# A hybrid attention and RG-LRU block on one core: where weight subtractions and key projections stand in the attention

## Chip, core and metric

One Trainium2 chip, one of its cores. The metric is the device time of one execution in microseconds (us). Each time is a median over runs; the profile is one execution of its own.

## What is computed

One trunk layer in float32, for 512 tokens of width 1024, 16 heads of width 64 and a feed-forward width of 2816:

```python
xn = rmsnorm(h, norm_mix_g)
u = einsum('bsd,de->bse', xn, w_in)
q, k, v, xr, gr, ga, gb = split(u, 7 parts of 1024)
ya = chunked_band_attention(q, k, v, rel_table) @ w_attn_out
xc = causal_depthwise_conv(xr, conv_w, conv_b)
hr = rg_lru(xc, w_rg_r, b_rg_r, w_rg_i, b_rg_i, rg_lambda)
yb = (hr * gelu(gr)) @ w_rnn_out
g_a, g_b = split(sigmoid(concat([ga, gb]) + b_merge))
h = h + (g_a * ya + g_b * yb) @ w_o
hn = rmsnorm(h, norm_ffn_g)
g, up = split(hn @ w_ffn_in)
h = h + (silu(g) * up) @ w_ffn_out
out = rmsnorm(h, final_norm_g)
```

## The kernel before

Every float32 operand of a matmul is split into a high and a low part: ScalarE copies the high part (L82), VectorE subtracts it from the source (L83), and each product is three matmuls (L76 to L78). Weights come from HBM into `raw` tiles by SyncE's queue (SP, L143), and are split into `whl` tiles. One chunk of weights, such as `qk3` (the columns of q and k of head pair 3) or `ga0` (two column blocks of gate A), is two loads and two splits, for rows 0 to 511 (`_0`) and 512 to 1023 (`_4`). There are four `whl` buffers, so room for two chunks: the splits of a chunk wait until the one before the last has been used up. The order of chunks is `plan`; a call of `weights` fetches one chunk ahead of the one it returns.

The stage in question is the attention. It goes through 16 heads, two to a pair. For head h, TensorE does, in this order, which is fixed by hand (`manual_schedule` for TensorE):

- `transposed(h)`: ten transposes of the probabilities `p` into `pT`, which are split into `pp`;
- `scores(h + 1)`: eight matmuls of `q` with the high and low keys `kh` and `kl`. VectorE adds the bias and takes the running minimum (L733), ScalarE takes exponentials (L734), VectorE the reciprocal `rl` of their sums (L735), and GpSimd scales the four blocks of `p` by it (L737);
- the projections that `laid[h]` names ahead of the bar;
- `weigh(h)`: eight matmuls of `pp` with the values, collected in `oacc`; after the second head of a pair the result is split into `aT`;
- the projections that `laid[h]` names behind the bar.

The projections are matmuls that need nothing from the softmax and fill its latency: `q_tile` and `k_tile` of the later pairs, and `gate_a`, the gate's columns. Each is 24 matmuls of 512 columns. The result of `k_tile` goes through two steps on ScalarE, one on VectorE and one on GpSimd for each head of the pair: `kh` (L693), `kl` (L694), and copies of both into the other half of the partitions (L695, L696).

Beside this, the stage prepares the feed-forward's Strassen-like block products: sums and differences of weight blocks are made once on VectorE and kept in HBM. `spill` loads four blocks of `w_ffn_out` (tiles `spill_a2` and `spill_a3`), subtracts them (L607) and stores them (L609, L611); `spill_in` does the like for two chunks of `w_ffn_in` (`spill_fg2`, `spill_fu2`, L632 to L636). The loop over heads takes one step of these generators per head, from head 2 on.

TensorE's order is written by hand. On the other engines and on SP's queue the order is set by a scheduler that models the time, and an instruction for which `keep_in_program_order` was called keeps its place in the written order against what is written around it. Before, that is said of the loads of these blocks alone, so the scheduler was free to put the subtractions elsewhere.

## Time and profile before

| what | value |
|---|---|
| time, median of 3 runs | 869.23 us (869.2 to 869.92) |
| time of the profiled execution | 870.58 us |
| its span | 868.6 us |
| mean granted TensorE clock | 0.991 |
| TensorE busy | 847.8 us, 98% of the span |
| VectorE busy | 676.7 us, 78% |
| ScalarE busy | 520.7 us, 60% |
| GpSimd busy | 116.7 us, 13% |
| DMA | 147.23 MB, 169 GB/s |

A row of the list of waits reads: engine, what waits, line, `<-` the one it waits for: total us, times, longest us. In a timeline a row is start, duration, engine, line, operation, out<-in, shape, count, and in brackets the idle time before it and what ended it. Names are those of tiles in the code, with the numbers left out (`spill_a` is `spill_a2` and `spill_a3`).

### The profile page before, as it was taken

To read this page: it belongs to the slowest core of one execution; us is meant where nothing else is said; L and a number is where in the kernel's file an instruction comes from. 1 tells how busy PE (TensorE), PEld (TensorE's weight loads), DVE (VectorE), ACT (ScalarE), POOL (GpSimd) and SP (SyncE) were. 2 spreads that over 40 slices of the span, in tenths; PEclk is the share of its full clock that TensorE was granted. 3 is DMA by queue.
4 is the path that set the end of the run, shared out by engine and by line. 5 is a ranking of instruction groups with operands and counts; after the bars stand their busy time and mean duration, and the time that the engine had idled before them with its cause. 6 is when DMAs were issued, how large, how long until landed. Compare 5 with 4: busy or idle time off the path is not lost.

```text
span 868.6 us, 13104 instructions
## 1 busy us (share of the span) xinstructions
PE 847.8 (98%) x4860; PEld 740.7 (85%) x4860; DVE 676.7 (78%) x1006; ACT 520.7 (60%) x893; POOL 116.7 (13%) x152
## 2 busy tenths in 40 slices
PE   8999999999997799999999999999999999999997
PEld 6977887888885688888888889999999999988885
DVE  5789766798677766565658886989999887689985
ACT  7578677625564667666654456655565565385454
POOL 2323302210021424231200000000000001000002
PEclk9999999999998899999999999999999999999999
DMA  8684333684677622232337461365766232886622
GB/s 271 205 304 146 97 97 95 223 331 152 194 225 267 197 64 86 72 111 72 99 110 248 153 216 49 120 238 163 254 207 238 94 122 98 282 291 207 215 72 97
DMA packets 107599, 147.23 MB, mean 169 GB/s; under 512 B 7184, under 2 KB 77440, under 8 KB 107536
## 3 DMA queue, kind: packets, MB, share of 16 engines
q1 hardware_dynamic: 103856, 138.74, 48.6%
q10 hardware_dynamic: 3680, 7.67, 2.9%
q8 instruction: 38, 0.62, 0.3%
q14 instruction: 25, 0.20, 0.1%
HBM read 123.27 MB, written 23.11 MB: 169 GB/s over the span
## 4 chain that ended last, share of the span: by engine, by line
PE 92%; DMA 3%; ACT 2%; DVE 1%; issue 1%; POOL 1%; SPq 0%; ACTq 0%; POOLq 0%; DVEq 0%
PE po_out L76 4%; PE po_out L77 4%; PE po_out L78 4%; PE p_fu L78 2%; PE p_fg L78 2%; PE p_fu L76 2%; PE p_fg L76 2%; PE p_fg L77 2%; PE p_fu L77 2%; PE o L768 2%; PE po_gb L76 2%; PE po_gb L77 2%; PE po_ga L76 2%; PE po_ga L78 2%; PE po_ya L76 2%; PE po_gb L78 2%
## 5 line engine op out<-in xcount | busy, mean ns | idle before, releaser
L737 POOL TENSOR_SCALAR p<-p,rl 128x128 f32<-128x128 f32 (+1 forms) x64 | 44.6, 714 | 104.1 <-DVE rl L735 104.0
L1223 POOL TENSOR_TENSOR act_lo<-act,act_hi 128x1024 fp32r<-128x1024 f32 x1 | 2.4, 2407 | 294.3 <-ACT act_hi L1222 294.3
L734 ACT ACTIVATE p<-p,m 128x128 f32<-128x128 f32 (+1 forms) x64 | 35.7, 563 | 9.1 <-DVE m L733 9.1
L83 DVE TENSOR_TENSOR pp<-pT,pp 128x384 fp32r<-128x384 f32 (+1 forms) x48 | 27.7, 596 | 13.9 <-ACT pp L82 13.8
L83 DVE TENSOR_TENSOR whl_t<-raw_t,whl_t 128x1024 fp32r<-128x1024 f32 x26 | 31.9, 1228 | 0.3 <-ACT whl_t L82 0.3
L733 DVE CUSTOM_DVE_ANT_0 p<-s,bias 128x128 f32<-128x128 f32 (+1 forms) x64 | 29.0, 484 | 1.9 <-PE s L730 1.8
L729 PE MATMUL s<-kh,q 128*128 128x128 f32 (+1 forms) x64 | 22.1, 366 | 7.9 <-ACT kh L695 7.9
L76 PE MATMUL po_gr<-xnT,whl_gr 128*128 128x512 f32 (+1 forms) x80 | 28.2, 353 | 0.1
L82 ACT ACTIVATE whl_t<-raw_t 128x1024 fp32r<-128x1024 f32 x26 | 27.2, 1046 | 1.5 <-PE po_h L78 1.5
L77 PE MATMUL po_xr<-xnT,whl_xr 128*128 128x512 f32 (+1 forms) x80 | 27.8, 353 | 0.0
L77 PE MATMUL po_gr<-xnT,whl_gr 128*128 128x512 f32 (+1 forms) x80 | 27.6, 346 | 0.0
L78 PE MATMUL po_gr<-xnT,whl_gr 128*128 128x512 f32 (+1 forms) x80 | 27.5, 348 | 0.0
L78 PE MATMUL po_xr<-xnT,whl_xr 128*128 128x512 f32 (+1 forms) x80 | 27.3, 346 | 0.0
L76 PE MATMUL po_xr<-xnT,whl_xr 128*128 128x512 f32 (+1 forms) x80 | 26.7, 352 | 0.6 <-ACT xnT L358 0.6
L83 DVE TENSOR_TENSOR whl_fg_s<-s_fg,whl_fg_s 128x1024 fp32r<-128x1024 f32 x20 | 24.4, 1223 | 2.9 <-ACT whl_fg_s L82 2.9
L83 DVE TENSOR_TENSOR whl_fu_s<-s_fu,whl_fu_s 128x1024 fp32r<-128x1024 f32 x20 | 24.4, 1222 | 2.9 <-ACT whl_fu_s L82 2.9
L76 PE MATMUL po_q<-xnT,whl_qk 128*128 128x512 f32 x64 | 26.2, 409 | 0.0
L77 PE MATMUL po_q<-xnT,whl_qk 128*128 128x512 f32 x64 | 25.8, 403 | 0.0
L82 ACT ACTIVATE whl_fu_s<-s_fu 128x1024 fp32r<-128x1024 f32 x20 | 21.0, 1056 | 7.8 <-PE q_fu L78 2.6
L78 PE MATMUL po_q<-xnT,whl_qk 128*128 128x512 f32 x64 | 25.7, 401 | 0.0
L76 PE MATMUL po_gb<-xnT,whl_gb 128*128 128x512 f32 x64 | 25.3, 395 | 0.2 <-DVE xc L497 0.2
L748 PE MATMUL pT<-ident,p 128*128 128x128 f32 x160 | 21.9, 277 | 3.6 <-POOL p L737 3.5
(472 smaller groups left out, 3306.2 us busy)
## 6 DMA issues: line engine op xcount, KB each, us to landing
raw_fg<-in_w_ffn_in_dram SPq DMA_DIRECT2D x22, 512.0 KB, 3.8
raw_fu<-in_w_ffn_in_dram SPq DMA_DIRECT2D x22, 512.0 KB, 3.6
raw_t<-sums SPq DMA_DIRECT2D x20, 512.0 KB, 4.2
raw_qk<-in_w_in_dram SPq DMA_DIRECT2D x32, 256.0 KB, 3.1
raw_b<-in_w_ffn_out_dram SPq DMA_DIRECT2D x15, 512.0 KB, 4.8
spillf<-in_w_ffn_out_dram SPq DMA_DIRECT2D x12, 512.0 KB, 8.4
sums<-spillf SPq DMA_DIRECT2D x12, 512.0 KB, 3.7
raw_xr<-in_w_in_dram SPq DMA_DIRECT2D x8, 512.0 KB, 4.8
```

Of the source, the lines that this page charges most:

```text
L76: pe.matmul(o, sh, mh, start=start, stop=False, skip_group_check=parts)
L77: pe.matmul(o, sh, ml, start=False, stop=False, skip_group_check=parts)
L78: pe.matmul(o, sl, mh, start=False, stop=stop, skip_group_check=parts)
L82: act.activation(hi, src, AF.Copy)
L83: dve.tensor_sub(lo, src, f(hi))
L729: pe.matmul(scs[qb], qs, kh[:, e, 0:w], start=True, stop=False)
L733: dve.tensor_tensor_reduce(prob[qb][:], scs[qb], bias[:, S - w:S], -1.0, 3e38, ALU.add, ALU.min, nmax[:, qb:qb + 1])
L734: act.activation(prob[qb][:], prob[qb][:], AF.Exp, bias=nmax[:, qb:qb + 1], scale=-1.0, accum_out=lsum[:, qb:qb + 1])
L737: pool.tensor_scalar(prob[qb][:], prob[qb][:], rl[:, qb:qb + 1], 1.0, ALU.mult, ALU.mult)
L748: pe.transpose(pt[:, at * P:(at + 1) * P], prob[qb][:, kb * P:(kb + 1) * P], ident[:])
L768: pe.matmul(po[:, S - n:S], st, pp[i][:, part, lo:lo + n], start=kb == 0 and part == 0, stop=kb == NT - 1 and part == 1)
L1223: pool.tensor_sub(lo[:], o[:], f(hi[:]))
```

## The change

Three things. The subtractions of the feed-forward weights keep their written place on VectorE, and the loop gives each generator its own heads (`steps_at`): the loads of `w_ffn_out` at head 1, its four subtractions at heads 3 to 6; the loads of fg2 at head 6 and of fu2 at head 7, their sums at heads 7 and 8, and 9 and 10. The list of projections has q2 behind head 0 and every key projection one head sooner; gates take up the places that come free at the end. The order of weight chunks has `ga2` after `qk7` instead of after `qk6`, to fit the list.

```diff
-        for at, n in ((5, 0), (6, 2), (7, 4), (7, 6)):
+        for at, n in ((5, 0), (7, 2), (7, 4), (7, 6)):
...
-            dve.tensor_sub(out_, a_, b_)
+            in_order(dve.tensor_sub(out_, a_, b_), pinned and w is w_ffn_out)
...
-    def spill_in(name, both):
+    def spill_in(name, at):
         col = chunks[index[name]][1][0][1]
+        both = big(at, [P, 2, 4, CW], F32, f"spill_{name}")
...
         yield
-        dve.tensor_add(s1, s3, s1)
+        in_order(dve.tensor_add(s1, s3, s1), True)
         dve.tensor_sub(s3, s2, s3)
         yield
-        dve.tensor_sub(s2, s1, s2)
+        in_order(dve.tensor_sub(s2, s1, s2), True)
         dve.tensor_sub(s4, s4, s2)
...
-    laid = ("q1 k1 |", "q2 |", "k2 |", "q3 |", "k3 |", "q4 |", "k4 |", "q5 | g0",
-            "k5 | g1", "q6 |", "k6 | g2", "q7 | g3", "k7 | g4", "g5 |", "g6 |", "g7 |")
+    laid = ("q1 k1 | q2", "k2 |", "q3 |", "k3 |", "q4 |", "k4 |", "q5 |", "k5 | g0",
+            "q6 | g1", "k6 |", "q7 |", "k7 | g2", "g3 |", "g4 |", "g5 |", "g6 | g7")
...
-        yield from spill_in("fg2", big(2, [P, 2, 4, CW], F32, "spill_fg2"))
-        yield from spill_in("fu2", big(3, [P, 2, 4, CW], F32, "spill_fu2"))
-
-    spilling = spills()
+
+    spilling = {n: steps for n, steps in enumerate((spills(), spill_in("fg2", 2), spill_in("fu2", 3)))}
+    steps_at = {1: (0,), 3: (0,), 4: (0,), 5: (0,), 6: (0, 1), 7: (2, 1), 8: (1,), 9: (2,), 10: (2,)}
...
-            if h > 1:
-                next(spilling, None)
+            for n in steps_at.get(h, ()):
+                next(spilling[n], None)
```

What this does to the order shows in three places. A number behind a name is that of a head (`p4`, `rl4`), a pair (`q1`, `kl1`) or a tile, and the changed kernel's line numbers are one higher from the attention's functions on.

VectorE in head 0, from the reciprocal of head 1's softmax on. Before:

```order
L735 RECIPROCAL rl1_2321<-l1_2319 128x4
L607 TENSOR_TENSOR spill_a2_2551<-spill_a2_2551 128x1024
L683 SCALAR_TENSOR_TENSOR q1_2387<-po_q1_2350,q1_2387 64x512
L607 TENSOR_TENSOR spill_a2_2551<-spill_a3_2552,spill_a2_2551 128x1024
L683 SCALAR_TENSOR_TENSOR q1_2387<-po_q1_2350,q1_2387 64x512
L607 TENSOR_TENSOR spill_a3_2552<-spill_a3_2552,spill_a2_2551 128x1024
L83 TENSOR_TENSOR whl_qk3_0_2499<-raw_qk3_0_2496,whl_qk3_0_2499 128x1024
L607 TENSOR_TENSOR spill_a3_2552<-spill_a3_2552 128x1024
L694 TENSOR_TENSOR kl1_2418<-po_k1_2392,kh1_2417 64x512
```

The same place in the changed kernel:

```order
L736 RECIPROCAL rl1_2321<-l1_2319 128x4
L684 SCALAR_TENSOR_TENSOR q1_2387<-po_q1_2350,q1_2387 64x512 x2
L83 TENSOR_TENSOR whl_qk3_0_2443<-raw_qk3_0_2440,whl_qk3_0_2443 128x1024
L695 TENSOR_TENSOR kl1_2418<-po_k1_2392,kh1_2417 64x512
L83 TENSOR_TENSOR whl_qk3_4_2449<-raw_qk3_4_2446,whl_qk3_4_2449 128x1024
L771 TENSOR_TENSOR oacc0_2427<-o0_2428,oacc0_2427 64x512
L695 TENSOR_TENSOR kl1_2418<-po_k1_2392,kh1_2417 64x512
L684 SCALAR_TENSOR_TENSOR q2_2476<-po_q2_2439,q2_2476 64x512
```

The four subtractions L607 are gone from between q1 and k1.

VectorE where q3's results are taken over and the next score reductions begin. Before (head 4, p5):

```order
L683 SCALAR_TENSOR_TENSOR q3_2754<-po_q3_2717,q3_2754 64x512
L770 TENSOR_TENSOR oacc1_2648<-o3_2759,oacc1_2648 64x512
L683 SCALAR_TENSOR_TENSOR q3_2754<-po_q3_2717,q3_2754 64x512
L733 ISA p5_0_2802,m5_2800<-s5_0_2806,bias5_2683 128x128
L733 ISA m5_2800 128x1
```

In the changed kernel (head 3, p4):

```order
L684 SCALAR_TENSOR_TENSOR q3_2685<-po_q3_2648,q3_2685 64x512
L771 TENSOR_TENSOR oacc1_2690<-o2_2691,oacc1_2690 64x512
L607 TENSOR_TENSOR spill_a2_2481<-spill_a2_2481 128x1024
L684 SCALAR_TENSOR_TENSOR q3_2685<-po_q3_2648,q3_2685 64x512
L734 ISA p4_0_2731,m4_2729<-s4_0_2735,bias4_2614 128x128
```

The first subtraction now stands here, ahead of q3's second half and of the reductions.

The end of the same softmax, on VectorE before:

```order
L83 TENSOR_TENSOR pp4_2_2776<-pT4_2_2790,pp4_2_2776 128x384
L83 TENSOR_TENSOR aT0_2548<-oacc1_2648,aT0_2548 128x512
L735 RECIPROCAL rl5_2801<-l5_2799 128x4
L83 TENSOR_TENSOR whl_qk5_0_2940<-raw_qk5_0_2937,whl_qk5_0_2940 128x1024
L694 TENSOR_TENSOR kl3_2856<-po_k3_2830,kh3_2855 64x512
```

and on VectorE in the changed kernel:

```order
L734 ISA p4_3_2734,m4_2729<-s4_2_2737,bias4_2614 128x512
L734 ISA m4_2729 128x1
L83 TENSOR_TENSOR pp3_2_2705<-pT3_2_2719,pp3_2_2705 128x384
L83 TENSOR_TENSOR whl_qk5_0_2869<-raw_qk5_0_2866,whl_qk5_0_2869 128x1024
L736 RECIPROCAL rl4_2730<-l4_2728 128x4
L695 TENSOR_TENSOR kl3_2785<-po_k3_2759,kh3_2784 64x512
```

with ScalarE at that place in the changed kernel:

```order
L735 ACTIVATE p4_2_2733,l4_2728<-p4_2_2733,m4_2729 128x384
L82 ACTIVATE whl_qk5_0_2869<-raw_qk5_0_2866 128x1024
L735 ACTIVATE p4_3_2734,l4_2728<-p4_3_2734,m4_2729 128x512
L434 DMA bias6_2831<-ext_d_391 128x512
L694 ACTIVATE kh3_2784<-po_k3_2759 64x512
```

The first half of the split of qk5 has moved from behind the reciprocal to ahead of it, and on ScalarE, where it stood behind the last exponential, to ahead of that. The same stands before `rl6`, with ga0 in qk5's place.

## The prediction

> **What bounds the kernel now.** I read the page first, for the share of each engine and for the slices in which TensorE is not full.

> ```profile
> span 868.6 us, 13104 instructions
> PE 847.8 (98%) x4860; PEld 740.7 (85%) x4860; DVE 676.7 (78%) x1006; ACT 520.7 (60%) x893; POOL 116.7 (13%) x152
> PE   8999999999997799999999999999999999999997
> PEclk9999999999998899999999999999999999999999
> ```

> TensorE is the bound, and its granted clock is full except in slices 12 and 13, about 261 to 304 us, where it also idles. The list of waits says for whom it idles there; the third row is VectorE's.

> ```profile
> PE s L729 <- ACT kh L695: 7.9, 4, 5.9
> PE pT L748 <- POOL p L737: 3.5, 5, 2.1
> DVE spill_a L607 <- DMA spill_a<-in_w_ffn_out_dram: 6.5, 2, 5.7
> ```

> So TensorE waits 11.4 us in the attention, for keys (`kh`) and for scaled probabilities (`p`). A table of stretches, cut at each head's first transpose and where the clock changes, prices the whole damage (columns: stretch, length, busy time of PE, PEld, DVE, ACT, POOL, PEclk, DMA share, GB/s).

> ```profile
> 264.04:271.24 7.20, 1.28 (x12) 1.05 (x11) 6.77 (x7) 5.23 (x10) 0.61 (x1) 0.89 0.67 246
> 271.24:276.60 5.36, 4.85 (x14) 4.05 (x15) 5.02 (x14) 2.58 (x9) 1.54 (x2) 0.51 0.98 320
> 276.60:282.13 5.53, 5.53 (x29) 4.67 (x27) 2.64 (x5) 1.36 (x4) 1.73 (x3) 1.00 0.72 222
> 282.13:292.45 10.32, 9.51 (x53) 7.95 (x52) 9.41 (x21) 7.42 (x17) 3.77 (x5) 1.00 0.78 240
> 292.45:298.17 5.72, 1.95 (x12) 1.13 (x12) 4.09 (x7) 2.71 (x6) 4.29 (x5) 0.89 0.86 252
> 298.17:303.67 5.50, 5.50 (x16) 4.63 (x16) 3.21 (x12) 3.96 (x11) 1.28 (x3) 0.50 0.20 66
> 303.67:308.82 5.15, 5.15 (x26) 4.37 (x25) 0.39 (x1) 0.59 (x1) 1.53 (x4) 0.99 0.07 22
> 308.82:317.90 9.08, 9.08 (x52) 7.95 (x52) 7.37 (x18) 7.32 (x17) 2.66 (x4) 1.00 0.11 29
> 317.90:327.77 9.87, 9.46 (x53) 7.95 (x52) 7.05 (x17) 7.29 (x17) 3.42 (x8) 1.00 0.45 136
> 327.77:336.90 9.13, 9.13 (x52) 7.92 (x52) 7.37 (x18) 7.32 (x17) 3.16 (x6) 1.00 0.09 29
> ```

> A head with one projection and no wait takes 9.1 us (rows 308.82 and 327.77). Head 1 takes 18.09 (264.04 to 282.13), head 2 10.32, head 3 16.37 (292.45 to 308.82), head 5 9.87. The losses are 9.0, 1.2, 7.3 and 0.8, and another 0.8 at head 7 by the same kind of wait: **19.1 us**. The waits listed above are 11.4 of them; most of the rest is the half clock (0.51, 0.50) that follows each of the two long pauses.

> Why head 1 waits is in the rows of VectorE, with the ScalarE step and the TensorE rows that follow.

> ```profile
> 255.71 0.18 DVE L735 RECIPROCAL rl<-l 128x4 f32<-128x4 f32 x1
> 261.54 1.23 DVE L607 TENSOR_TENSOR spill_a<-spill_a 128x1024 f32<-128x1024 f32 x1 [5.65 <-DMA spill_a<-in_w_ffn_out_dram]
> 264.37 1.23 DVE L607 TENSOR_TENSOR spill_a<-spill_a,spill_a 128x1024 f32<-128x1024 f32 x1 [0.90 <-DMA spill_a<-in_w_ffn_out_dram]
> 268.63 1.22 DVE L607 TENSOR_TENSOR spill_a<-spill_a 128x1024 f32<-128x1024 f32 x1
> 269.88 0.68 DVE L694 TENSOR_TENSOR kl<-po_k,kh 64x512 fp32r<-64x512 f32 x1
> 270.60 0.59 ACT L695 ACTIVATE kh<-po_k 64x512 fp32r<-64x512 f32 x1 [1.85 <-DVE kl L694]
> 264.04 1.28 PE L748 MATMUL pT<-ident,p 128*128 128x128 f32 x10
> 271.24 0.47 PE L729 MATMUL s<-kh,q 128*128 128x128 f32 x1 [5.92 <-ACT kh L695]
> ```

> The first weight subtraction stands at the head of VectorE's queue and waits 5.65 us for its load. Behind it stand q1, then k1; the four subtractions are mixed among them. `kl` comes at 269.88, the other half of `kh` at 270.60, and the scores of head 2 at 271.24.

> **The change part by part.** *The subtractions.* The changed order has none of L607 before head 3, 40 VectorE rows later; no instruction is removed. In head 0, k1's `kl` then follows q1 and one weight split. In the clean head below, the first half of the keys is ready 3.0 us after the projection ends (weigh starts 316.69, scores released 319.71).

> ```profile
> 310.99 0.40 PE L730 MATMUL s<-kl,q 128*128 128x512 f32 x1
> 316.69 1.37 PE L768 MATMUL o<-pp,v 128*128 128x512 f32 x8
> 317.90 1.40 PE L748 MATMUL pT<-ident,p 128*128 128x128 f32 x10
> 319.71 0.33 PE L729 MATMUL s<-kh,q 128*128 128x128 f32 x1 [0.41 <-ACT kh L695]
> ```

> *The projections.* q2 now stands between head 0's weigh and head 1's transposes, and each later key projection comes a head earlier. One projection is 5.5 us of TensorE (from after 310.99 to 316.69), weigh 1.2, transposes 1.0: head 2's scores come 7.7 us after k1's end, against the 3.0 that keys need. From k2 on a whole head lies between. Every `kh` wait goes: heads 1, 5 and 7, and the 1.07 us part of head 3. The count of projections is unchanged at 22, so TensorE's busy work is unchanged: zero. g6 and g7 share head 15; nothing waits there, since gate work has no successor in the attention.

> *Queues.* The loads of `spill_a` keep their place in SP's queue, after the two qk3 loads; what moves past are the stores, which now stand among later qk and ga loads and wait for the subtraction of their head. The tightest such load is the second half of qk7, behind the fg2 stores of head 8 and wanted in head 10, a head of about 15 us and one of 9 later; cost zero by that cover. The fg2 load is issued after head 6's last subtraction and its sum stands before `rl8`. Before, that sum ran 9.0 us after its load was issued; even then head 7's two projections (11 us) cover it.

> *What is late next.* The subtractions now stand inside heads 3 to 6, which have no spare VectorE time ahead of the softmax. The clean head shows how tight it is (VectorE's first score reduction and reciprocal, ScalarE's and VectorE's weight split, GpSimd's scaling of four `p`).

> ```profile
> 311.09 0.29 DVE L733 CUSTOM_DVE_ANT_0 p<-s,bias 128x128 f32<-128x128 f32 x1
> 314.87 0.17 DVE L735 RECIPROCAL rl<-l 128x4 f32<-128x4 f32 x1
> 314.70 1.04 ACT L82 ACTIVATE whl_qk<-raw_qk 128x1024 fp32r<-128x1024 f32 x1
> 315.78 1.35 DVE L83 TENSOR_TENSOR whl_qk<-raw_qk,whl_qk 128x1024 fp32r<-128x1024 f32 x1 [0.74 <-ACT whl_qk L82]
> 290.32 5.73 POOL L737 TENSOR_SCALAR p<-p,rl 128x128 f32<-128x128 f32 x4 [6.49 <-DVE rl L735]
> 303.00 2.05 POOL L737 TENSOR_SCALAR p<-p,rl 128x128 f32<-128x128 f32 x4 [2.87 <-DVE rl L735]
> 315.24 3.02 POOL L737 TENSOR_SCALAR p<-p,rl 128x128 f32<-128x128 f32 x4 [9.97 <-DVE rl L735]
> ```

> Counted from that head's start (308.82), `rl` runs at 6.05, `p` from 6.4 to 9.4, and the next transposes start at 9.08 and want the last `p` 0.3 later. There is no slack. In head 3 of the changed order a subtraction (1.23) stands before the score reductions of p4, and both halves of the split of qk5 stand before `rl4`: ScalarE's 1.04 ahead of the last exponential, VectorE's ahead of `rl4`. One after the other they cost about 1.1, since the exponential runs beside VectorE's half. So `rl4` comes at 6.05 + 1.23 + 1.1 = 8.4, and `p` is done between 10.8 (2.05 of scaling) and 11.8 (3.02, a split beside it), against 9.4 wanted: 1.4 to 2.4, I take **1.9**. Head 5 has the same pattern before `rl6` (a subtraction, then the split of ga0): **1.9**. In heads 4 and 6 the subtraction also stands before `rl`, but TensorE is itself 1.9 late: 0 to 0.5 each, taken 0.1. In head 10 a kl (0.68) and an fu2 subtraction (half of the 1.23, by its half size) stand before `rl11`: 0.3 to 0.9, taken **0.6**. Head 2 has a kl there: 0.1. Sum 4.7, ends 3.1 and 7.

> GpSimd's scaling takes 2.05 with VectorE idle, 3.02 with one split beside it, 5.73 among splits and subtractions. [...]

> *Sum.* −19.1 + 4.7 = −14.4 us. The profiled execution took 870.58 (span 868.6 and 1.98 around it), 1.35 over the median of the runs, 869.23. On the profiled one that makes 856.2, on the median 854.8; I say **855.0**.

> **The rivals.** *Full clearing, 850.1.* The new waits vanish: 869.23 − 19.1. For it: 9.1 us heads exist with VectorE 7.4 busy, and 7.4 + 1.23 still fits in 9.1. Against it: the fit is one of throughput, and the order inside the head is what delays `rl`.

> *The clock drops again, 858 to 861.* The half clock began near the end of pauses of 7.2 us (264.04 to 271.24) and 5.7 us without a score or projection matmul, at mean 0.89. My two new pauses are 1.0 of transposes and 1.9 of wait, 2.9 us; head 2, with 1.2 us lost, kept 1.00. The truth lies between. A drop lasts 5.4 us at half clock in the rows and costs 2.7, and a bit more with its part in the pause: one 858, two 861. [...]

> *Keys of pair 1 stay late, 864.* If VectorE reaches k1's `kl` more than 4.7 us later than worked out, the 9.0 of head 1 stays. The queue shown holds nothing that waits on a load there.

> *Slower, 876.* GpSimd's scaling is squeezed to 5.73 in each of the heads 3 to 6, as at 290.32: 3.7 more than 2.05 and a clock drop of 2.7 per head, 4 × 6.4 = 25.6 lost against 19.1 won. It decides when two or more two-input operations stand back to back right behind each `rl`; the new order mostly has a q or kl there, which waits for TensorE and leaves GpSimd a gap.

> *No effect.* The change does nothing if VectorE's order were not what holds the keys; 5.65 us of idle at its queue's head speaks against that.

> **How the numbers follow.** The worked sum (852 to 857.5) 0.52; full clearing 0.18; clock drops or waits twice as large (858 to 862.5) 0.18; late keys 0.04; no change to be measured 0.03; slower 0.05. About 0.2% is what a measurement of this kernel can tell from no change, here 1.7 us: faster 0.92, same 0.03, slower 0.05. The range 849 to 862.5 reaches from full clearing to two drops, 0.88 by these chances less what I may have mis-sized inside them.

> **What would show each step.** Right: no wait of VectorE on the loads of `spill_a`; no wait of the scores on `kh`; heads 1 and 2 near 9.1 us after their start; PEclk 1.00 through 261 to 304; the remaining waits are transposes on `p`, at heads 4 and 6, 1.4 to 2.4 each. Wrong: a wait of transposes in every head from 3 to 7, a 0.5 clock row behind one of them, scaling rows near 5 us, or the first scores of head 2 again waiting for `kh`. After the attention the rows should be the same, some 14 us earlier; if a load there arrives late instead, part of the gain is given back and the number is too low.

## The result and the profile after

The changed kernel takes 858.32 us (median of 4 runs, 858.28 to 858.36), the kernel before 869.22 us beside it. The ratio is 0.9874, with a 95% interval of 0.9857 to 0.9891: 10.9 us faster. The prediction said 855.0 us, with a range of 849.0 to 862.5. The profiled execution took 858.36 us, 12.2 less than that of before.

The head of the page, with TensorE's clock by slices, shows no slice with a lower clock any more, and the mean granted clock is 0.999 (0.991 before).

```profile
span 856.6 us, 13113 instructions
PE 843.3 (98%) x4860; PEld 736.7 (86%) x4860; DVE 678.4 (79%) x1006; ACT 519.6 (61%) x893; POOL 113.0 (13%) x152
PEclk9999999999999999999999999999999999999999
```

Of the list of waits, these are TensorE's rows in the attention. The rows `s <- kh` (7.9 us) and `spill_a <- DMA` (6.5 us) of before are gone. What is left is transposes that wait for `p`, and q projections that wait until `oacc` has been read out of the accumulator bank that they need. The two rows add up to 3.2 us, less than the losses below, since this list counts a wait from the end of the matmul before: one transpose has a row of 0.33 us, but ten in a run take 1.25 us.

```profile
PE pT L749 <- POOL p L738: 2.7, 9, 0.3
PE po_q L76 <- DVE oacc L771: 0.5, 2, 0.3
```

The table of stretches, cut at each head's first transpose (heads 1 to 7, then head 11; columns as before), prices what is left. A head without a wait takes 9.05 us with one projection and 14.55 with two.

```profile
269.79:278.81 9.02, 9.02 (x52) 7.92 (x50) 6.52 (x16) 6.79 (x16) 2.97 (x4) 1.00 0.10 29
278.81:288.42 9.61, 9.34 (x53) 7.87 (x52) 7.60 (x18) 7.43 (x18) 2.23 (x7) 1.00 0.47 138
288.42:298.63 10.21, 9.64 (x52) 8.02 (x52) 7.76 (x18) 7.04 (x16) 2.53 (x6) 1.00 0.23 80
298.63:308.36 9.73, 9.39 (x52) 7.96 (x52) 8.55 (x19) 7.64 (x18) 3.60 (x7) 1.00 0.52 163
308.36:318.63 10.27, 9.70 (x52) 8.02 (x52) 7.88 (x18) 6.93 (x16) 2.55 (x7) 1.00 0.38 107
318.63:328.56 9.93, 9.52 (x53) 7.96 (x52) 8.68 (x19) 7.56 (x18) 4.31 (x8) 1.00 0.51 143
328.56:343.85 15.29, 14.95 (x76) 12.46 (x76) 13.21 (x25) 10.33 (x21) 6.79 (x10) 1.00 0.95 294
377.09:393.08 15.99, 15.30 (x77) 12.58 (x76) 10.97 (x21) 10.33 (x21) 6.01 (x10) 1.00 0.37 105
```

Head 1 is now clean (18.09 before). Heads 3 to 7 lose 1.2, 0.7, 1.2, 0.9 and 0.7 us, heads 2 and 10 lose 0.6 each, head 11 loses 1.4: 7.3 in all. By the same count the kernel before lost 19.4, and 19.4 − 7.3 = 12.1 is nearly the whole difference between the two profiles, 12.2.

Head 3 was forecast clean but for 0.1 us. This is the end of the softmax before it: VectorE's reciprocal, then GpSimd's queue, then the transposes that wait.

```profile
286.24 0.17 DVE L736 RECIPROCAL rl<-l 128x4 f32<-128x4 f32 x1
287.51 0.15 POOL L435 MEMSET bias<- 64x64 f32 x1 [3.37 <-DMA bias<-ext_d]
287.75 2.05 POOL L738 TENSOR_SCALAR p<-p,rl 128x128 f32<-128x128 f32 x4
289.19 0.33 PE L749 MATMUL pT<-ident,p 128*128 128x128 f32 x1 [0.23 <-POOL p L738]
289.86 0.98 PE L749 MATMUL pT<-ident,p 128*128 128x128 f32 x7 [0.34 <-POOL p L738]
```

`rl` was there at 286.24, and the scaling could have begun some 0.4 us later, as it did in the kernel before (`rl` at 314.87, scaling at 315.24). It began at 287.75, because the fill of a corner of the next bias tile (L435) stands ahead of it in GpSimd's queue and waited 3.37 us for that tile's load. A fill stands before head 11's `p` too, though there the profile names VectorE's L637, a sum of fu2, as what ended its wait:

```profile
375.48 0.17 DVE L736 RECIPROCAL rl<-l 128x4 f32<-128x4 f32 x1
376.42 0.15 POOL L435 MEMSET bias<- 64x64 f32 x1 [3.65 <-DVE spill_fu L637]
376.66 2.05 POOL L738 TENSOR_SCALAR p<-p,rl 128x128 f32<-128x128 f32 x4
```

### The profile page after: what moved, and what is told of

Same layout as the page of the kernel before. It is cut to its first block, busy times and chain, and to the rows that moved or that the text cites. A ratio compares the mean times of both kernels' runs of the same rounds, so it can differ in the third digit from the quotient of the medians.

```text
span 856.6 us, 13113 instructions
## 1 busy us (share of the span) xinstructions
PE 843.3 (98%) x4860; PEld 736.7 (86%) x4860; DVE 678.4 (79%) x1006; ACT 519.6 (61%) x893; POOL 113.0 (13%) x152
## 4 chain that ended last, share of the span: by engine, by line
PE 91%; DVE 3%; ACT 2%; DMA 1%; POOL 1%; issue 1%; ACTq 0%; SPq 0%; POOLq 0%; DVEq 0%
PE po_out L76 4%; PE po_out L78 4%; PE po_out L77 4%; PE p_fu L78 2%; PE p_fg L78 2%; PE p_fg L76 2%; PE p_fu L76 2%; PE p_fu L77 2%; PE p_fg L77 2%; PE po_gb L76 2%; PE po_gb L77 2%; PE po_ga L76 2%; PE pT L749 2%; PE po_ga L78 2%; PE po_k L76 2%; PE po_k L78 2%
## 5 line engine op out<-in xcount | busy, mean ns | idle before, releaser
L738 POOL TENSOR_SCALAR p<-p,rl 128x128 f32<-128x128 f32 (+1 forms) x64 | 40.0, 642 | 89.3 <-DVE rl L736 82.1
L735 ACT ACTIVATE p<-p,m 128x128 f32<-128x128 f32 (+1 forms) x64 | 35.6, 560 | 12.7 <-DVE m L734 12.7
L83 DVE TENSOR_TENSOR whl_t<-raw_t,whl_t 128x1024 fp32r<-128x1024 f32 x26 | 31.6, 1216 | 1.2 <-ACT whl_t L82 1.2
L83 DVE TENSOR_TENSOR pp<-pT,pp 128x384 fp32r<-128x384 f32 (+1 forms) x48 | 27.2, 594 | 4.0 <-ACT pp L82 3.9
L82 ACT ACTIVATE whl_t<-raw_t 128x1024 fp32r<-128x1024 f32 x26 | 27.1, 1046 | 1.5 <-PE po_h L78 1.5
L83 DVE TENSOR_TENSOR whl_qk<-raw_qk,whl_qk 128x1024 fp32r<-128x1024 f32 x16 | 20.8, 1302 | 8.0 <-ACT whl_qk L82 6.5
L83 DVE TENSOR_TENSOR whl_fg_s<-s_fg,whl_fg_s 128x1024 fp32r<-128x1024 f32 x20 | 24.4, 1220 | 3.0 <-ACT whl_fg_s L82 3.0
L83 DVE TENSOR_TENSOR whl_fu_s<-s_fu,whl_fu_s 128x1024 fp32r<-128x1024 f32 x20 | 24.3, 1221 | 2.9 <-ACT whl_fu_s L82 2.9
L82 ACT ACTIVATE whl_fu_s<-s_fu 128x1024 fp32r<-128x1024 f32 x20 | 21.0, 1056 | 8.0 <-PE q_fu L78 2.6
L76 PE MATMUL po_q<-xnT,whl_qk 128*128 128x512 f32 x64 | 25.3, 395 | 0.5 <-DVE oacc L771 0.5
L76 PE MATMUL po_gb<-xnT,whl_gb 128*128 128x512 f32 x64 | 25.3, 395 | 0.2 <-DVE xc L497 0.2
L76 PE MATMUL po_ga<-xnT,whl_ga 128*128 128x512 f32 x64 | 25.3, 395 | 0.0
L77 PE MATMUL po_gb<-xnT,whl_gb 128*128 128x512 f32 x64 | 25.2, 393 | 0.0
```

The source lines that it names most:

```text
L76: pe.matmul(o, sh, mh, start=start, stop=False, skip_group_check=parts)
L77: pe.matmul(o, sh, ml, start=False, stop=False, skip_group_check=parts)
L82: act.activation(hi, src, AF.Copy)
L83: dve.tensor_sub(lo, src, f(hi))
L735: act.activation(prob[qb][:], prob[qb][:], AF.Exp, bias=nmax[:, qb:qb + 1], scale=-1.0, accum_out=lsum[:, qb:qb + 1])
L738: pool.tensor_scalar(prob[qb][:], prob[qb][:], rl[:, qb:qb + 1], 1.0, ALU.mult, ALU.mult)
```

## The experiments

This table holds, for every kernel, what each head loses against 9.05 or 14.55 us. It is worked out from the starts of the first transposes in the profiled execution. The profiled time less the sum lies between 850.5 and 852.1 us for all thirteen, so these heads account for nearly all differences. Heads left out lose under 0.1; "other" is heads 8 and on without 11. The ratios below are to the kernel before, measured beside each kernel on the same chip; the chips differ, and a difference of 1 or 2 us between kernels from different chips is not certain (the changed kernel itself took 858.32 us and, on another chip, 860.89).

| kernel | profiled us | h1 | h2 | h3 | h4 | h5 | h6 | h7 | h11 | other | sum |
|---|---|---|---|---|---|---|---|---|---|---|---|
| before | 870.58 | 9.0 | 1.3 | 7.3 | 0.0 | 0.8 | 0.1 | 0.9 | 0.0 | 0.0 | 19.4 |
| after | 858.36 | 0.0 | 0.6 | 1.2 | 0.7 | 1.2 | 0.9 | 0.7 | 1.4 | 0.6 | 7.3 |
| pins alone | 859.66 | 0.8 | 0.0 | 0.8 | 1.2 | 1.4 | 0.4 | 3.9 | 0.0 | 0.0 | 8.5 |
| list alone | 866.61 | 2.2 | 6.2 | 0.6 | 2.4 | 0.0 | 0.7 | 1.4 | 1.4 | 0.6 | 15.5 |
| fill behind | 858.95 | 0.0 | 0.6 | 0.0 | 3.7 | 0.0 | 2.1 | 0.0 | 1.0 | 0.6 | 8.0 |
| no subtractions | 857.28 | 0.0 | 0.3 | 1.2 | 0.6 | 0.0 | 0.7 | 1.2 | 1.4 | 0.9 | 6.3 |
| splits behind | 865.09 | 0.0 | 0.0 | 1.8 | 0.0 | 2.8 | 0.0 | 3.3 | 4.3 | 2.2 | 14.4 |
| fill and splits behind | 868.96 | 0.0 | 0.6 | 4.3 | 1.2 | 4.3 | 1.5 | 1.4 | 3.5 | 1.7 | 18.5 |
| no subtractions, fill behind | 853.76 | 0.0 | 0.6 | 0.0 | 0.6 | 0.0 | 0.6 | 0.1 | 0.3 | 0.6 | 2.8 |
| two early, fill behind | 854.54 | 0.0 | 0.6 | 0.0 | 0.7 | 0.0 | 0.6 | 0.0 | 0.4 | 0.6 | 2.9 |
| four early, fill behind | 858.58 | 0.6 | 3.7 | 0.0 | 0.6 | 0.0 | 0.6 | 0.1 | 0.3 | 0.6 | 6.5 |
| four early, fill free | 863.48 | 0.6 | 4.0 | 0.0 | 0.7 | 1.2 | 0.6 | 1.2 | 3.4 | 1.0 | 12.6 |
| two early, fill behind, old list | 858.23 | 1.6 | 3.0 | 0.8 | 0.0 | 0.8 | 0.1 | 0.9 | 0.0 | 0.0 | 7.2 |

**The pins alone.** The changed kernel with `laid` and the order of chunks of before.

```diff
-    laid = ("q1 k1 | q2", "k2 |", "q3 |", "k3 |", "q4 |", "k4 |", "q5 |", "k5 | g0", ...
+    laid = ("q1 k1 |", "q2 |", "k2 |", "q3 |", "k3 |", "q4 |", "k4 |", "q5 | g0", ...
...
```

> Only the pinned subtractions with their heads; the old list of projections and order of chunks. Theory (both parts are needed; VectorE's blocked queue was the larger loss): the 5.65 us block and both half clocks go, the wait for keys stays at about 0.8 us in heads 1, 3, 5 and 7 (3.2 us), and the subtractions cost some 5 us of waits for probabilities in heads 3 to 6: 858.5 to 861. Rival (the list is what does it): 866 or more, with the keys of pair 1 still late by several us.

Measured: 859.09 us, ratio to the kernel before 0.9887 (0.9872 to 0.9901). Head 1 falls from 18.09 to 9.85 us, head 3 from 16.37 to 9.88:

```profile
263.98:273.83 9.85, 9.32 (x53) 7.98 (x52) 6.90 (x17) 7.28 (x17) 3.15 (x6) 1.00 0.43 131
282.90:292.78 9.88, 9.46 (x53) 7.96 (x52) 8.17 (x18) 7.29 (x17) 2.29 (x6) 1.00 0.54 172
```

So what the scheduler did with the subtractions and sums, with the half clock behind it, was nearly all of the loss, and the pins with their heads remove it without the list: at head 1 the stop at VectorE's queue, at head 3 the sums of fu2, which before stood around that head's reciprocal. Head 7 loses 3.9 here, a stretch of half clock among it (326.68 to 330.09).

**The list alone.** The kernel before with the new `laid` and order of chunks, and nothing else.

```diff
-    laid = ("q1 k1 |", "q2 |", "k2 |", "q3 |", "k3 |", "q4 |", "k4 |", "q5 | g0", ...
+    laid = ("q1 k1 | q2", "k2 |", "q3 |", "k3 |", "q4 |", "k4 |", "q5 |", "k5 | g0", ...
...
```

> Only the new list of projections and order of chunks; the subtractions placed by the scheduler as before. Theory: VectorE still waits 5.6 us for the load in head 0, but q2 now fills 5.5 us of what TensorE idled, so head 1 loses 1 to 3 us instead of 9.0; the fg2 and fu2 sums stay in heads 2 and 3 and squeeze GpSimd's scaling there (2 to 5 us): 860 to 866. Rival (the blocked queue alone decides): 866 or more. Rival (the list alone suffices): 859 or less.

Measured: 867.77 us, ratio 0.999 (0.998 to 0.9999), hardly faster than before and above the theory's 866. The first rival's bound holds, but not by its reason: the waits for keys are gone, and TensorE waits 7.7 us for `p` instead. VectorE's subtractions and splits now stand right behind a reciprocal, and GpSimd's scaling takes 5.84 us there instead of 2.05. The rows are TensorE's wait, then VectorE's, GpSimd's, and a transpose of head 2.

```profile
PE pT L748 <- POOL p L737: 7.7, 12, 2.2
278.26 0.69 DVE L632 TENSOR_TENSOR spill_fg<-spill_fg 128x512 f32<-128x512 f32 x1 [0.31 <-issue]
278.87 0.17 DVE L735 RECIPROCAL rl<-l 128x4 f32<-128x4 f32 x1
278.99 0.69 DVE L633 TENSOR_TENSOR spill_fg<-spill_fg 128x512 f32<-128x512 f32 x1
279.60 1.22 DVE L83 TENSOR_TENSOR whl_qk<-raw_qk,whl_qk 128x1024 fp32r<-128x1024 f32 x1
280.74 0.78 DVE L635 TENSOR_TENSOR spill_fg<-spill_fg 128x512 f32<-128x512 f32 x1
279.24 5.84 POOL L737 TENSOR_SCALAR p<-p,rl 128x128 f32<-128x128 f32 x4 [6.59 <-DVE rl L735]
284.47 0.47 PE L748 MATMUL pT<-ident,p 128*128 128x128 f32 x1 [2.23 <-POOL p L737]
```

This is the mechanism of the prediction's "slower" rival, here in the kernel without the pins. In the changed kernel no four scalings took over 3.4 us.

**The fill behind the scaling.** The changed kernel; the next bias tile's load and fill are written behind the scaling of `p`, and the fill is kept there.

```diff
-        pool.memset(b[64:128, 448:512], NEG)
+        in_order(pool.memset(b[64:128, 448:512], NEG), late)
...
             pool.tensor_scalar(prob[qb][:], prob[qb][:], rl[:, qb:qb + 1], 1.0, ALU.mult, ALU.mult)
+        if h + 1 < HEADS:
+            biases.append(bias_tile(h + 1, True))
```

> The changed kernel with GpSimd's fill of the next bias tile written behind the scaling of p and pinned there. Theory (the fill of bias5 and that of bias13, which the scheduler moved ahead of the scaling of p3 and p11, wait for their load and hold the scaling 1.1 and 0.8 us): heads 3 and 11 lose that much less, 856.2 to 857.0 against 858.3. Rival (the scaling would come as late for another reason, the reciprocal or VectorE beside it): 858.0 to 858.5.

Measured: 857.49 us, ratio 0.9873 (0.9858 to 0.9887); the profiled execution took 858.95. The time lies between the theory's range and the rival's, and is hardly below the changed kernel's. Head 3 is clean now, so its wait was the fill's. Head 11 still loses 1.0 of its 1.4, so there the fill was the smaller part. Heads 4 and 6 lose 3.7 and 2.1, and heads 5 and 7 nothing: the pattern that the prediction drew. The 3.7 is about 2.0 of wait and 1.7 of clock, by an estimate that has 3.41 us at half clock cost half their length: in the kernel before, the matmuls of a q projection came every 0.43 us at half clock (300.68 to 303.24) and every 0.23 us right behind it. The rows are the stretches of heads 3 and 4, the half clock inside head 4, and the last transposes of head 4.

```profile
288.29:297.34 9.05, 9.05 (x53) 7.95 (x52) 7.77 (x18) 6.91 (x16) 1.07 (x4) 1.00 0.23 87
297.34:310.12 12.78, 11.22 (x53) 9.52 (x52) 8.48 (x19) 7.59 (x18) 5.84 (x11) 0.87 0.51 146
300.00:303.20 3.20, 3.20 (x15) 3.10 (x14) 2.58 (x8) 3.01 (x8) 1.05 (x2) 0.51 0.57 165
299.74 1.51 PE L749 MATMUL pT<-ident,p 128*128 128x128 f32 x7 [1.33 <-POOL p L736]
```

So in the changed kernel the fill's wait at head 3 did not add to the others. The reading that fits both tables is that it let TensorE run late, and that the subtractions' delay was spread over heads 3 to 7.

**Without the subtractions.** The changed kernel without the twelve sums and differences of the weights in the attention (loads and stores remain).

```diff
-            in_order(dve.tensor_sub(out_, a_, b_), pinned and w is w_ffn_out)
+            if not (pinned and w is w_ffn_out):
+                dve.tensor_sub(out_, a_, b_)
...
```

> The changed kernel without the twelve subtractions and additions of feed-forward weights in the attention (the weight sums are left out of the computation; their loads and stores stay). Theory (the subtractions ahead of the reciprocals cost the waits for p in heads 4 to 7 and part of that of head 11): 0.65 + 1.2 + 0.85 + 0.7 + 0.6 = 4.0 us less, 854 to 855. Rival (the weight splits that stand ahead of the reciprocals, or the fills on GpSimd, are the cause): 857 or more.

Measured: 857.77 us, ratio 0.9879 (0.9861 to 0.9898), a miss: the rival's 857 or more held. Heads 3 and 11 lose as much as with the subtractions, so there the fill alone is enough. At head 11 it takes both edits to clear most of the loss: 1.0 is left with the fill moved alone, 1.4 without the subtractions alone, 0.3 with both (below). The kernel could not say more: the scheduler, free to place the fills, put another one ahead of the scaling of head 7's `p`. The next kernel of this kind therefore fixes the fill too.

**The next three, beside the changed kernel again.** All four ran on one other chip.

> The changed kernel again, unaltered, as a reference for the three others on the same chip. Both theories: 858.3, within 0.5 us. Heads 3, 4, 5, 6 and 7 again lose 1.1, 0.7, 1.2, 0.9 and 0.7 us.

Measured: 860.89 us (858.61 to 862.99), ratio 0.9913 (0.99 to 0.9927). Two of the five runs, at 862.99 and 862.19, show a granted clock of 0.994 and 0.997 instead of 0.998 or 0.999; why the median run, 860.89 at 0.999, is 2.3 above the lowest stays open. The profiled one (858.61) repeats the head table within 0.2 us.

*Splits behind the reciprocal.* ScalarE's and VectorE's halves of the split keep their written place for the chunks from `qk4` on and for the gates.

```diff
+        ins = act.activation(hi, src, AF.Copy), dve.tensor_sub(lo, src, f(hi))
+        for i in ins if late else ():
+            tc.keep_in_program_order(i)
...
```

> The changed kernel, with the splits of the chunks from qk4 on and of the gates kept in their written place on ScalarE and VectorE, which is behind the reciprocal. Theory A (a split, 1.04 on ScalarE, and a subtraction, 1.23, both ahead of the reciprocal make the waits; the fill of the bias tile ahead of the scaling makes those of heads 3 and 11): heads 4 and 6 lose 1 us less together, heads 3 and 11 still lose 1.1 and 1.4, time 856 to 857.7. Theory B (the subtraction alone uses up the slack of heads 3 to 6, wherever the split stands): 858 or more.

Measured: 867.02 us, ratio 0.9978 (0.9968 to 0.9988), 6.1 more than the changed kernel beside it. Theory A fell. Theory B's bound holds, but its reason, the subtraction alone, explains no loss on top. Heads 3, 5 and 7, before which the scaling takes 4.08 us with two splits beside it, lose 1.8 to 3.3; heads 4 and 6 nothing. *With the fill behind as well*, both edits together:

> The changed kernel with both the fill of the next bias tile behind the scaling of the probabilities and the splits behind the reciprocal. Theory A: the waits of 2.5 and 2.1 us that stood at heads 4 and 6 with the fill moved alone fall to about 1.2 each, the subtraction's own 1.23; time 854.5 to 856. Theory B: they stay over 2, time about 857.5.

Measured: 869.92 us, ratio 1.0007 (0.9994 to 1.002), a miss of both theories. Splits behind the reciprocal are not free; they run beside GpSimd's scaling and lengthen it. The rows are the reciprocal of head 3's softmax and VectorE's work behind it, with GpSimd's scaling, first with the splits behind, then with fill and splits behind.

```profile
285.01 0.18 DVE L737 RECIPROCAL rl<-l 128x4 f32<-128x4 f32 x1
285.96 2.46 DVE L82 TENSOR_TENSOR whl_qk<-raw_qk,whl_qk 128x1024 fp32r<-128x1024 f32 x2 [0.77 <-ACT whl_qk L82]
285.39 4.08 POOL L739 TENSOR_SCALAR p<-p,rl 128x128 f32<-128x128 f32 x4 [3.05 <-DVE rl L737]
```

```profile
285.27 2.35 DVE L82 TENSOR_TENSOR whl_qk<-raw_qk,whl_qk 128x1024 fp32r<-128x1024 f32 x2
288.96 1.21 DVE L608 TENSOR_TENSOR spill_a<-spill_a 128x1024 f32<-128x1024 f32 x1
285.54 5.19 POOL L737 TENSOR_SCALAR p<-p,rl 128x128 f32<-128x128 f32 x4 [2.90 <-DVE rl L735]
```

Four scalings took 2.05 us alone, 3.02 with one split or subtraction of 1.2 us beside them on VectorE, 4.08 with two, 5.19 with three: 0.97 to 1.11 more for each.

*Without the subtractions, fill behind.* The two edits together:

```diff
-            in_order(dve.tensor_sub(out_, a_, b_), pinned and w is w_ffn_out)
+            if not (pinned and w is w_ffn_out):
+                dve.tensor_sub(out_, a_, b_)
...
+        in_order(pool.memset(b[64:128, 448:512], NEG), late)
```

> The changed kernel with the fill of the bias tile behind the scaling, and with the twelve weight sums and differences inside the attention left out of the computation (loads and stores remain). In this order the splits also stand behind the reciprocals. Theory A: heads 3 to 7 lose nothing, 4.5 us less than the changed kernel; what is left is the bank waits of heads 2 and 10 and something in head 11: 852.5 to 854.5. Theory B (something else than subtraction, split and fill fills those heads): 857 or more.

Measured: 853.74 us (853.71 to 853.8), ratio 0.9824 (0.9812 to 0.9837), as theory A had it. Heads 3, 5 and 7 are clean, and heads 4 and 6 lose only the 0.6 of a bank. In this kernel one split still stands beside the scaling of head 4's `p` (3.02 us) and costs nothing. The rows are VectorE's and GpSimd's in the timeline, and then the only one of TensorE's waits in the attention that is left.

```profile
294.27 0.18 DVE L731 RECIPROCAL rl<-l 128x4 f32<-128x4 f32 x1 [0.41 <-ACT p L730]
294.64 3.02 POOL L733 TENSOR_SCALAR p<-p,rl 128x128 f32<-128x128 f32 x4 [5.86 <-DVE rl L731]
```

```profile
PE po_q L76 <- DVE oacc L768: 1.2, 4, 0.3
```

So the head's slack holds one split beside the scaling. A second split beside it cost head 3 1.8 (splits behind); a subtraction and a split ahead of the reciprocal, with one split beside the scaling, cost head 6 2.1 (fill behind). Without the subtractions the scheduler also put those splits back behind the reciprocal, so the 2.1 is for the subtraction with the split that it moved; the runs do not part the two.

**The subtractions in heads that have room.** With the fill behind, two of the four subtractions stand between head 0's weigh and q2 (three projections), two in head 7, the sums of fg2 in head 8 and those of fu2 in head 11 (two projections each).

```diff
-    steps_at = {1: (0,), 3: (0,), 4: (0,), 5: (0,), 6: (0, 1), 7: (2, 1), 8: (1,), 9: (2,), 10: (2,)}
+    steps_at = {0: (0,), 7: (0, 0, 1), 8: (1, 1), 9: (2,), 11: (2, 2)}
+    mid_at = {0: (0, 0)}
...
             weigh(h, pp)
+            for n in mid_at.get(h, ()):
+                next(spilling[n], None)
```

> The changed kernel with the fill of the bias tile behind the scaling, and the subtractions taken out of the heads with one projection: two of w_ffn_out between head 0's weigh and q2, two in head 7, the sums of fg2 in head 8 and those of fu2 in head 11 (heads 7, 8 and 11 have two projections). Theory A (VectorE has no room ahead of the reciprocal in heads 3 to 6, and has it in heads 0, 7, 8 and 11): heads 3 to 6 lose nothing, at most 2 us are lost in heads 1, 2 and 8 together, 853.5 to 855.5. Theory B (the subtractions cost their time wherever they stand in the attention): 857 or more.

Measured: 853.87 us (853.75 to 854.79), ratio 0.9834 (0.9821 to 0.9847). This computes everything and comes as low as the kernel without the subtractions. No wait for `p` is left in TensorE's list. VectorE's rows in head 0 show the two subtractions in time that was idle in the changed kernel, neither waiting for its load.

```profile
267.52 1.20 DVE L607 TENSOR_TENSOR spill_a<-spill_a 128x1024 f32<-128x1024 f32 x1
268.75 0.69 DVE L695 TENSOR_TENSOR kl<-po_k,kh 64x512 fp32r<-64x512 f32 x1
269.48 1.23 DVE L607 TENSOR_TENSOR spill_a<-spill_a,spill_a 128x1024 f32<-128x1024 f32 x1
271.29 0.69 DVE L684 SCALAR_TENSOR_TENSOR q<-po_q,q 64x512 fp32r<-64x512 f32 x1 [0.59 <-ACT q L683]
```

*All four in head 0*, with fg2 in heads 7 and 8:

```diff
-    steps_at = {0: (0,), 7: (0, 0, 1), 8: (1, 1), 9: (2,), 11: (2, 2)}
-    mid_at = {0: (0, 0)}
+    steps_at = {0: (0,), 6: (1,), 7: (1,), 8: (1, 2), 11: (2, 2)}
+    mid_at = {0: (0, 0, 0, 0)}
```

> The same with all four subtractions of w_ffn_out between head 0's weigh and q2 (4.9 us of VectorE, which sat idle 8.4 us between 256 and 271 us in the changed kernel). Theory A: heads 3 to 7 lose nothing, but the last of the four stands ahead of head 2's score reductions, so up to 2.5 us are lost at head 2: 853.5 to 856.5. Theory B: 857 or more.

Measured: 858.30 us, ratio 0.9882 (0.987 to 0.9895), against 853.5 to 856.5 of theory A. The place was right, head 2, the size was not: 3.7 us instead of up to 2.5, since the granted clock was 0.50 from 282.50 to 285.91. TensorE had work from 283.07 on, so that cost about 1.4, and the wait alone was about 2.3. *The same with the fill left free:*

```diff
-        in_order(pool.memset(b[64:128, 448:512], NEG), late)
+        pool.memset(b[64:128, 448:512], NEG)
...
```

> As the one with four early subtractions, but with the fill of the bias tile left to the scheduler, which again puts some fills (bias tiles of heads 3, 7, 9, 13) ahead of a scaling. Theory A: a fill ahead of a scaling waits for its load and costs 1 to 1.5 us in those heads that have no slack: 1 to 3 us more than with the fill behind. Rival: the loads are in time by then and it is no slower.

Measured: 863.65 us, ratio 0.9945 (0.9925 to 0.9966), 5.3 more, beyond the 1 to 3 of theory A. Heads 5, 7 and 11 lose 1.2, 1.2 and 3.4, each with a fill ahead of its scaling; the 3.4 has a stretch of half clock in it (382.12 to 385.53). So what a free fill costs depends on where the scheduler happens to put it.

**The list, with the other waits gone.** The version with two early subtractions, with the old list and order of chunks, the same edit as in the first experiment.

> The version with two early subtractions (853.87), with the list of projections and the order of chunks of the kernel before. It tells what the new list is worth once the subtractions and the fill are out of the way. Theory (the list takes away the rest of the waits for keys, which with the pins alone and the old list were 0.8 us each at heads 1, 3 and 5): the scores wait for keys in heads 1, 3, 5 and 7, 0.8 us each, and up to 1.2 more in head 1, where a subtraction stands between the two halves of k1's low keys: 856 to 859. Rival (the list is worth nothing, the order of VectorE alone decides): 853 to 854.7.

Measured: 857.60 us, ratio 0.9863 (0.9846 to 0.9879), in the theory's range: by the medians the list is worth 3.7 us there. The waits for keys come back at heads 1, 3, 5 and 7, 0.8 each. Head 2 loses 3.0 to late `p`, which was not expected: with this list the second subtraction stands among the reductions of that head's scores, and 1.7 of the 3.0 is, at half its length, a stretch of half clock (276.51 to 279.92).

```profile
PE s L728 <- ACT kh L696: 1.9, 4, 0.5
PE pT L749 <- POOL p L736: 1.2, 3, 0.6
271.20 1.22 DVE L607 TENSOR_TENSOR spill_a<-spill_a,spill_a 128x1024 f32<-128x1024 f32 x1
```

## Why the prediction held, and where it was off

- **The loss of before.** The step "first weight subtraction at the head of VectorE's queue" is shown by the pins alone: head 1 went from 18.09 to 9.85 us. Head 1 and the clock through 261 to 304 us came out as written, head 2 but for 0.6. For most of head 3's 7.3 us the prediction named no step that removes it; with the pins alone, which take the sums of fu2 away from there, it is 0.8, and the scaling takes 3.02 us instead of 5.73.
- **The projections.** No score waits for `kh` in the changed kernel. In it, however, the list is worth 0.8 us by the medians (859.09 against 858.32), and the two ratios, 0.9887 and 0.9874, overlap in their intervals, so it can't be told from nothing: the time that the list frees goes back into waits for `p`. With the fill and the subtractions out of the way it is worth 3.7.
- **The new waits** were mis-sized: 4.7 forecast, 7.3 measured. The step that failed is "Head 2 has a kl there: 0.1", and with it the 0.6 of head 10: heads 3 and 11 lost 1.2 and 1.4. The prediction followed VectorE's order and never GpSimd's, where the fill stood ahead of the scaling; that was all of head 3's loss and about 0.5 of head 11's. The 1.9 each at heads 4 and 6 came out as 0.7 and 0.9, and the 0.1 at heads 5 and 7 as 1.2 and 0.7. That is the prediction's own first sign of being wrong, a wait in every head from 3 to 7. With the fill out of the way there were about 2.0 and 2.1 of wait at heads 4 and 6 and none at 5 and 7: the mechanism was right, and the fill blurred it. The bank waits of heads 2 and 10, 0.6 each, were not in the sum. By heads the 2.6 too little is 1.1 at head 3, 0.8 at head 11 and 1.2 of banks, less 0.5 that heads 4 to 7 lost less than forecast.
- **The base.** 19.1 us of loss was read from an execution 1.35 us slower than the median, then taken off the median too. On the profiled basis the forecast was 856.2 against 858.36, which is 2.2 short, close to the 2.6 of the waits. On the median it was 854.8 against 858.32, and the rest of that miss is the base.
- **The rivals.** The clock did not drop in the profiled execution, though the time, 858.32, is the "one 858" of that rival: other losses made it up. That the clock held is in part luck. The forecast had pauses of 2.9 us and charged no drop for them; no run shows that for a pause of this length: up to 2.8 us none had half clock, and one of 3.04 had it. As it came, no pause in the changed kernel's attention was longer than 2.4, and with the fill behind, where the forecast pauses stood as drawn, head 4 lost the clock (0.51 from 300.00 to 303.20). On the second chip two of five runs of the changed kernel show a lower clock and 862 to 863 us, so that rival occurs in some runs. GpSimd squeezed to over 5 us did not occur in the changed kernel, though it did with the list alone and with fill and splits behind.
- **Queues.** No load of weights held TensorE up in the attention, as forecast (VectorE waited 1.2 us for one of qk3 and 0.3 for one of fg2). The load that cost time was a bias tile's, in ScalarE's queue, which the prediction did not follow.

## What to carry to other kernels

Here an instruction that waited for a load held back what stood behind it on its engine (VectorE's first subtraction 5.65 us in the kernel before, GpSimd's fill 3.37 us in the changed one), so follow the order of every engine on the path, GpSimd's small fills too, before a head is called clean. Side work goes into the stretches where the bound engine has the most work to itself; in a stretch without slack it costs its time ahead of the critical step, and beside it where it lengthens that step, as two of VectorE's splits lengthened GpSimd's scaling from 2.05 to 4.08 us. A gain read from a profile should be taken off that profile's own time.

## What was unexpected of the hardware

The half clock does not follow from the length of a pause alone. Counted from a head's first transpose to its first score, heads with 3.04, 3.09, 3.23, 3.56 and 4.09 us, among others, had half clock in the pause or behind it, and heads with 3.17, 3.46, 3.81 and 4.27 us had none; up to 2.8 us, none had it in these traces.

```profile
306.02:309.43 3.41, 1.75 (x12) 1.40 (x10) 2.61 (x4) 2.97 (x4) 3.12 (x3) 1.00 0.49 143
309.43:312.84 3.41, 2.73 (x18) 2.40 (x19) 3.38 (x7) 1.95 (x4) 1.11 (x3) 1.00 0.87 267
378.71:382.12 3.41, 2.17 (x11) 1.38 (x10) 2.22 (x4) 1.78 (x3) 2.50 (x5) 1.00 0.01 4
382.12:385.53 3.41, 3.07 (x14) 3.08 (x15) 0.77 (x4) 1.58 (x3) 0.28 (x1) 0.50 0.28 82
```

Why the clock held behind 1.75 us of work and dropped behind 2.17 stays open.

Long pauses also went with uneven times. With the fill behind, three of the four runs took 857.33 to 857.53 us at a granted clock of 0.998 or 0.999, and the one with the drop 858.95 at 0.996, so the same order has the drop in one execution and not in others. The two kernels whose heads lose at most 0.7 us each ran within 0.1 and 1.0 us of themselves (853.71 to 853.8, and 853.75 to 854.79); with fill and splits behind, which paused most, the runs lay between 866.11 and 872.45, with granted clocks from 0.989 to 0.997.
